# Sixteen projection blocks as seven products of quarter sums, in a stage of their own ahead of the pooling

## The chip, the cores and the metric

The kernel runs on one core of a Trainium2 chip. The metric is the device time of one execution in microseconds (us), from inputs in the chip's memory to the output there. Times are medians of several executions; a profile is one more execution, recorded by the hardware.

A core has TensorE (PE, matrix products into PSUM banks), VectorE (DVE), ScalarE (ACT), GpSimd (POOL) and SyncE (SP, which here issues all transfers). PEld is PE's loading of the stationary operand. An engine runs its own instructions in order and waits on semaphores for the others.

## What is computed

One transformer-like block over 1024 tokens of 1024 channels, with 16 learned meta tokens in front:

```python
u = rmsnorm(h, norm_mix)
z = u @ w_in                                   # 4112 columns
a, q, k, v, r, lr, ga, gb = split(z)           # 512, 256, 256, 512, 512, 16, 1024, 1024
p = (multiscale_pool(a) @ w_pool_mix) * pool_scale     # trailing means over 2, 4, 8, 16 tokens
y_a = p @ w_pool_out
log_a = log_sigmoid(lr @ w_gate_up + b_gate) / 16
o = gla_chunked(q / 8, k, v, log_a)            # gated linear attention, chunks of 64
y_b = (rmsnorm(o, gla_norm) * silu(r)) @ w_gla_out
m = sigmoid(ga) * y_a + sigmoid(gb) * y_b
h = h + m @ w_out
h = h + square(relu(rmsnorm(h, norm_ffn) @ w_ff1)) @ w_ff2
out = rmsnorm(h, norm_final)[16:]
```

## The kernel before

**Products.** Operands are float32, split into a rounded high part (an ACT copy) and a low part (a DVE subtraction). `mm3` makes one product from three matmuls per 128 rows of contraction: high x high, high x low, low x high. A direct block is 128 columns of a weight matrix against 512 tokens of either half: 8 x 3 matmuls for each half, 48 in all. Weight blocks come through the ring `W1`: `Ring.top_up` loads the next block into one of two raw buffers and splits it into one of two slots (`w1h`, `w1l`, each 1024 wide) as soon as the block that held the slot is done.

**Stages.** `start` (L368) normalizes eight tiles of 128 tokens and transposes them with PE (L239) into `TH`, `TL`, which hold the normalized tokens, channels on partitions, high and low, in two halves of 512 tokens (the meta tokens lead the first). The v projection of each tile (`v_tile`, 24 matmuls of 272 columns, with the 16 columns of lr) is woven in. Then come the pooling stage (four `a_block`, four `mix_block`, eight direct `ga_block`, four `ya_block` that multiply by the gates), the attention (`gla`), the output projection, and the two MLP layers.

**Attention.** `gla` runs four units (two pairs of heads, two halves). Each unit has a log decay (L659), six levels of masked scores (L707, a group of small matmuls; operands Q from DVE L732 and K from POOL L731, both times an exponential E from ACT; running sums in L674 and L675; the result merged by DVE L741) and then a state update across chunks. This chain uses PE little, so `pour` puts matmuls of a list of direct blocks, `fill`, between its steps: for every us that a step is expected to take, `PACE` us of filler. The filler before: k and q (2 blocks each), the second half of v, r (4), gb (8), and half of the GLA output projection.

**Seven products.** The first MLP layer already makes its blocks in pairs, 256 weight columns against all 1024 tokens, as a 2 x 2 by 2 x 2 product of quarters with seven quarter products in place of eight (the Strassen-Winograd scheme): P1, P2 on plain quarters, the other five on sums. A quarter product is 4 x 3 matmuls of 512 columns.

**Order.** PE's instructions stay in the order in which the code issues them. Those of the other engines are ordered by the scheduler of the framework.

## Time and profile before

| | us |
|---|---|
| median of 3 executions | 1280.34 (1279.92 to 1281.8) |
| the profiled execution | 1280.39 |
| its span in the profile | 1278.6 |

The page of the profile gives busy time by engine over the span, then the span in 40 slices, the chain of work that ended last, and groups of instructions that share a line, an engine and operands. In a group's row, "out<-in xcount | busy us, mean ns | idle before". PE's share in the chain that ended last is 85%, DVE's 5%. A matmul's duration overlaps its successor's, so PE's rate is read from starts or from busy time over count.

The slices that show where PE and DVE are busy (tenths, 40 slices of 32 us):

```profile
PE   5999999998999999999999999999999999999997
DVE  6446222262657664852797677677674777887686
ACT  6334334332355654430665445545553444444544
```

### The profile page before, as it was taken

The page shows a single profiled execution, that of the slowest core. Times are in us where ns is not written, and L with a number is a line of the kernel's source. Part 1 is how long each engine was busy: PE and PEld are TensorE (multiplying, and loading weights), DVE is VectorE, ACT ScalarE, POOL GpSimd, SP SyncE. Part 2 cuts the span into 40 slices and gives each one's busy share as a digit, 9 for nine tenths or more (in the row PEclk, how much of TensorE's full clock was granted, in tenths as well). Part 3 has the DMA queues.
Part 4 walks back from the last instruction along what each step waited for, and adds up shares of the span by engine and source line. Part 5 has one row for each costly group of instructions (what it writes and reads, how often), then busy time and mean ns, then how long its engine had stood idle before and what let it go on. Part 6 is the DMA issues. An engine that isn't in the chain of part 4 may idle for free.

```text
span 1278.6 us, 18111 instructions
## 1 busy us (share of the span) xinstructions
PE 1240.4 (97%) x6895; PEld 1020.3 (80%) x6895; DVE 798.5 (62%) x1295; ACT 590.5 (46%) x1045; POOL 78.8 (6%) x56
## 2 busy tenths in 40 slices
PE   5999999998999999999999999999999999999997
PEld 4988888887777788778878888888878788888776
DVE  6446222262657664852797677677674777887686
ACT  6334334332355654430665445545553444444544
POOL 1000001021111210520000000000000000000000
PEclk9999999998999999999999999999999999999999
DMA  8111223210032324880225445435559863333432
GB/s 237 49 33 50 83 83 100 67 33 17 26 108 89 103 93 129 272 308 31 84 99 175 159 130 165 160 130 165 167 196 355 288 239 108 99 91 91 166 92 90
DMA packets 138103, 164.92 MB, mean 129 GB/s; under 512 B 10368, under 2 KB 82832, under 8 KB 138016
## 3 DMA queue, kind: packets, MB, share of 16 engines
q1 hardware_dynamic: 138016, 163.76, 40.0%
q8 instruction: 54, 0.88, 0.3%
q14 instruction: 33, 0.27, 0.1%
HBM read 115.50 MB, written 48.23 MB: 128 GB/s over the span
## 4 chain that ended last, share of the span: by engine, by line
PE 85%; DVE 5%; issue 3%; DMA 3%; ACT 2%; POOL 0%; SPq 0%; DVEq 0%; POOLq 0%; ACTq 0%
PE b_mm L251 13%; PE b_mm L252 12%; PE b_mm L253 12%; PE b_o L252 8%; PE b_o L253 8%; PE b_o L251 8%; PE b_y L251 3%; PE b_y L253 3%; PE b_y L252 3%; PE b_sc L251 2%; PE b_sc L253 2%; PE b_z L251 2%; PE b_sc L252 2%; PE b_z L253 2%; PE b_z L252 2%
## 5 line engine op out<-in xcount | busy, mean ns | idle before, releaser
L251 PE MATMUL b_mm<-th,w1h 128*128 128x512 f32 (+1 forms) x496 | 188.4, 380 | 0.0
L252 PE MATMUL b_mm<-tl,w1h 128*128 128x512 f32 (+1 forms) x496 | 185.2, 373 | 0.0
L253 PE MATMUL b_mm<-th,w1l 128*128 128x512 f32 (+1 forms) x496 | 184.6, 372 | 0.0
L251 PEld LDWEIGHTS b_mm<-th,w1h 128*128 128x128 f32 x496 | 93.6, 189 | 20.9 <-issue 3.5
L76 DVE TENSOR_TENSOR w1l<-raw,w1h 128x1024 fp32r<-128x1024 f32 x38 | 50.7, 1335 | 91.4 <-ACT w1h L75 90.8
L253 PEld LDWEIGHTS b_mm<-th,w1l 128*128 128x128 f32 x496 | 93.7, 189 | 17.0
L252 PEld LDWEIGHTS b_mm<-tl,w1h 128*128 128x128 f32 x496 | 93.7, 189 | 15.5
L251 PE MATMUL b_o<-w1h 128*128 128x512 f32 x192 | 75.2, 392 | 2.7 <-DVE h L1154 1.7
L252 PE MATMUL b_o<-w1l,w1h 128*128 128x512 f32 x192 | 75.0, 391 | 1.2 <-DVE w1l L1008 1.2
L75 ACT ACTIVATE w1h<-raw 128x1024 fp32r<-128x1024 f32 x40 | 42.3, 1057 | 72.2 <-PE b_mm L252 72.2
L1007 ACT ACTIVATE w1h<-raw 128x512 fp32r<-128x512 f32 x88 | 54.7, 624 | 44.4 <-PE b_sc L252 14.1
L253 PE MATMUL b_o<-w1h,w1l 128*128 128x512 f32 x192 | 75.0, 391 | 0.1
L1008 DVE TENSOR_TENSOR w1l<-raw,w1h 128x512 fp32r<-128x512 f32 x88 | 60.2, 685 | 12.3 <-ACT w1h L1007 12.3
L483 DVE SCALAR_TENSOR_TENSOR t<-b_mm,t 128x512 f32<-128x512 f32 x40 | 27.6, 689 | 56.5 <-ACT t L482 56.1
L1202 DVE TENSOR_TENSOR bt<-w,w 128x512 f32<-128x512 f32 x80 | 54.8, 685 | 2.5 <-DMA w<-in_w_ff_dram 2.5
L1007 ACT ACTIVATE w1h<-bt 128x512 fp32r<-128x512 f32 x45 | 28.3, 630 | 57.1 <-issue 31.8
L251 PE MATMUL b_sc<-th,w1h 128*128 128x512 f32 x128 | 50.5, 394 | 0.7 <-ACT u2p L1126 0.7
L252 PE MATMUL b_o<-fxl,fxh 128*128 128x512 f32 x128 | 50.0, 391 | 0.7 <-DVE fxl L1008 0.7
L251 PE MATMUL b_mm<-wo,th 128*128 128x512 f32 x128 | 50.6, 396 | 0.0
L252 PE MATMUL b_z<-tl,w1h 128*128 128x512 f32 x128 | 49.9, 390 | 0.4 <-DVE tl L950 0.4
L251 PE MATMUL b_z<-th,w1h 128*128 128x512 f32 x128 | 49.9, 390 | 0.3 <-DVE h L1143 0.3
L253 PE MATMUL b_o<-fxh,fxl 128*128 128x512 f32 x128 | 50.2, 392 | 0.0
(289 smaller groups left out, 3072.6 us busy)
## 6 DMA issues: line engine op xcount, KB each, us to landing
hf_dram<-h SPq DMA_DIRECT2D x112, 256.0 KB, 2.1
raw<-hf_dram SPq DMA_DIRECT2D x112, 256.0 KB, 2.7
raw<-in_w_in_dram SPq DMA_DIRECT2D x32, 512.0 KB, 4.2
w<-in_w_ff_dram SPq DMA_DIRECT2D x64, 256.0 KB, 5.0
rawx<-in_w_ff_dram SPq DMA_DIRECT2D x16, 512.0 KB, 4.3
raw<-in_w_ff_dram SPq DMA_DIRECT2D x16, 512.0 KB, 4.2
xs<-in_x_dram SPq DMA_DIRECT2D x8, 512.0 KB, 5.7
ma_dram<-o SPq DMA_DIRECT2D x16, 256.0 KB, 2.0
```

The source lines that it names most:

```text
L75: self.nc.scalar.activation(hi, raw, ACT.Copy)
L76: self.eng.tensor_tensor(lo, raw, hi.bitcast(F32), ALU.subtract)
L251: pe.matmul(ps, ah, bh, start=first and i == 0, stop=False, skip_group_check=more)
L252: pe.matmul(ps, ah, bl, start=False, stop=False, skip_group_check=more)
L253: pe.matmul(ps, al, bh, start=False, stop=last and i == n - 1, skip_group_check=more)
L483: dve.scalar_tensor_tensor(t, b, 0.0, t, ALU.min, ALU.subtract)
L1007: act.activation(hi, a, ACT.Copy)
L1008: dve.tensor_tensor(lo, a, f32(hi), ALU.subtract)
L1202: dve.tensor_tensor(bt, w, S["w2"][q[3:]][:, i], ALU.add if q[2] == "+" else ALU.subtract)
```

## The change

The class `Quarters` now holds the seven-product scheme that the MLP's first layer had written out, with the weight blocks, their places and what is done with a result as arguments. It is used a second time, for sixteen blocks of `w_in`: all eight of ga, two of q, four of r and the first two of gb. They leave the pooling stage (ga) and the attention's filler (q, r, gb 0 and 1). Their results go to memory (`ga_dram`, `q_dram`, `r_dram`, `gb_dram`) and are loaded where they are used. P1, P2 of the first two pairs and v tiles are issued in `start`; the rest of the products in `gate_stage`, before the pooling.

The token side of five products needs differences of token quarters. `start` keeps a plain float32 copy `ut` of the transposed tiles (one more ACT copy from each transposed bank, L512), and `differences` makes the sums and their splits from these copies, 1024 columns an instruction.

In the pooling, the averages (`mean_block`) are parted from the mixing, groups run from 3 to 0, and the first `ya_block` starts with groups 3, 2, 1. `PACE` goes from 1.65 to 1.06, and POOL no longer splits weights in `start`.

```diff
-PACE, LEVEL = 1.65, 1.6
+PACE, LEVEL = 1.06, 1.6
-    banks(sc=1, mm=3, ms=3)
+    banks(sc=1, mm=2, ms=4)
...
+class Quarters:
+        def order(self):
+            for p, i in (("P1", 0), ("P2", 0), ("P1", 1), ("P2", 1), ("P5", 0), ("P5", 1)):
+                yield p, i
+            for p in ("P6", "P7", "P4", "P3"):
+                yield p, 0
+            for i in range(2, self.n + 1):
+                for p in ("P6", "P1", "P7", "P5", "P4", "P2", "P3"):
+                    m = i if p in ("P1", "P5", "P2") else i - 1
+                    if m < self.n:
+                        yield p, m
...
+        def prime(self):
+            w1 = [t.rearrange("p s (u c) -> p (s u) c", u=2) for t in (W1.hi, W1.lo)]
+            S["slots"] = [(w1[0][:, i], w1[1][:, i]) for i in range(4)]
+            self.made = ahead(self.forms(), 3)
...
+    BLOCKS = (
+        [("ga", d, C_GA + d * P) for d in range(8)] + [("q", p, C_Q + p * P) for p in range(2)]
+        + [("r", h, C_R + h * P) for h in range(HEADS)] + [("gb", d, C_GB + d * P) for d in range(2)]
+    )
...
+    def turned(u, t):
+        half, at = t // 4, OFF[t // 4] + (t % 4) * P
+        for j in range(2):
+            b = quad(bank("ms"))
+            for i in range(4):
+                pe.transpose(b[:, i], u[:, (4 * j + i) * P : (4 * j + i + 1) * P], ident)
+            k = slice(4 * j, 4 * j + 4)
+            split_from_psum(TH[half][:, k, at : at + P], TL[half][:, k, at : at + P], b)
+            act.activation(S["ut"][half, j][:, :, (t % 4) * P : (t % 4 + 1) * P], b, ACT.Copy)
...
     def start():
-        W1.eng = pool
+        for t in (1, 2, 3):
+            load(t)
+        q.load(0, 0)
         for t in range(8):
+            if t < 4:
+                layer_norm(xs[:, t % 4], us[:, t % 3])
+                turned(us[:, t % 3], t)
+                load(t + 4)
...
+                continue
+            if t == 4:
                 nc.sync.dma_start(xm, meta)
+                q.load(0, 1)
+                q.load(1, 1)
...
+                q.prime()
+                next(run)
+                next(run)
                 v_tile(0, 0)
+            layer_norm(xs[:, t % 4], us[:, t % 3])
+            turned(us[:, t % 3], t)
+            if t < 7:
+                v_tile(0, t - 3)
...
+        next(run)
         transposed(um, 0, 0)
+        next(run)
         v_tile(0, 8)
...
+    def halved(p, j):
+        h, l = gate_quarters.x[p] = [left.push(f"{p}{k}", [P, 4, HALF], F32R) for k in "hl"]
+        for k in range(0, 4, 2):
+            a = S["ut"][j][:, k : k + 2]
+            act.activation(h[:, k : k + 2], a, ACT.Copy)
+            dve.tensor_tensor(l[:, k : k + 2], a, f32(h[:, k : k + 2]), ALU.subtract)
+
+    def differences():
+        b11, b21, b12, b22 = (0, 0), (0, 1), (1, 0), (1, 1)
+        left.pop_to(S["left_x"])
+        differ(b11, b12, b11)
+        halved("P5", b11)
+        differ(b12, b22, b12)
+        differ(b22, b22, b11)
+        halved("P6", b22)
+        for t in range(4, 8):
+            v_tile(0, t)
+        lr_turn()
+        halved("P7", b12)
+        differ(b21, b21, b22)
+        halved("P4", b21)
...
+    def gate_result(i, w, b, u):
+        (kind, n, _), half = BLOCKS[2 * i + (w in (A12, A22))], int(w in (A21, A22))
+        if u is not None:
+            c = nxt("c")
+            dve.tensor_tensor(c, b, u, ALU.add)
+            b = c
+        o = nxt("o")
+        if kind == "q":
+            act.activation(o, b, ACT.Copy, scale=CH ** -0.5)
+            nc.sync.dma_start(q_dram[n, half], o)
+            return
+        t = sigmoid(b)
+        if kind == "r":
+            act.activation(t, t, ACT.Exp)
+            dve.scalar_tensor_tensor(o, b, gnorm[:, n : n + 1], t, ALU.mult, ALU.mult)
+            nc.sync.dma_start(r_dram[n, half], o)
+        else:
+            act.activation(o, t, ACT.Exp)
+            nc.sync.dma_start((ga_dram if kind == "ga" else gb_dram)[n, half], o)
...
-        (a_, 0), (a_, 1), (m_, 0), (a_, 2), (m_, 1), (a_, 3), (m_, 2), (g_, 0), (m_, 3), (g_, 1),
-        (y_, 0), (g_, 2), (g_, 3), (y_, 1), (g_, 4), (g_, 5), (y_, 2),
+        (a_, 3), (p_, 3), (a_, 2), (m_, 3), (p_, 2), (a_, 1), (m_, 2), (p_, 1), (a_, 0), (m_, 1), (p_, 0),
+        (y_, 0), (y_, 1), (y_, 2),
...
-        step(fill, q_block(p), W1, [w_cols(C_Q + p * P)])
-    for h in range(4):
-        step(fill, r_block(h), W1, [w_cols(C_R + h * P)])
-    for d in range(8):
+    for d in range(2, 8):
         step(fill, gb_block(d), W1, [w_cols(C_GB + d * P)])
```

Three places show how instructions move. First PE at the head of the program. Before, the first tile's eight transposes (into b_sc and b_ms) are followed by that tile's v matmuls (out b_mm, from the v weights vw and the tokens th, tl):

```order
L239 MATMUL b_sc<-ident,us 128x128 x4
L239 MATMUL b_ms<-ident,us 128x128 x4
L251 MATMUL b_mm<-vw_176,th_125 128x272
L252 MATMUL b_mm<-vw_176,th_125 128x272
L253 MATMUL b_mm<-vw_176,tl_129 128x272
```

Now the transposes of four tiles stand ahead of everything, and P1 of the first pair (out b_sc, weights w1h and w1l) follows:

```order
L509 MATMUL b_ms<-ident,us 128x128 x32
L253 MATMUL b_sc<-th_127,w1h 128x512
L254 MATMUL b_sc<-tl_131,w1h 128x512
L255 MATMUL b_sc<-th_127,w1l 128x512
L253 MATMUL b_sc<-th_127,w1h 128x512
```

24 matmuls of P1 and P2 moved ahead of the first v tile, and 24 transposes ahead of them. Behind them stand v tile 0, the transposes of tiles 4 to 7 with v tiles 1, 2, 3 between them, P1 and P2 of the second pair around the meta row's transposes, and v tiles 8, 4, 5, 6, 7.

Second, ACT where the first weight block of a direct projection is split (L75, from a raw buffer into w1h). Before, it stood inside the start, between the steps of a normalization (L225, L206) and the splits of a turned tile (L195):

```order
L225 ACTIVATE us,small<-xs 128x1024
L75 ACTIVATE w1h<-raw_109 128x1024
L206 ACTIVATE small<-small 128x1
L204 ACTIVATE small<-small 128x1
L351 ACTIVATE v_141<-b_mm 128x256
L195 ACTIVATE th_125<-b_sc 128x4x128
L75 ACTIVATE w1h<-raw_113 128x1024
```

Now it stands at the end of the products, among the sigmoids (L719 to L721, L626) of the last pair's results; raw_111 holds the first a-block's weights:

```order
L719 ACTIVATE t_851<-c 128x512
L720 ACTIVATE t_851<-t_851 128x512
L75 ACTIVATE w1h<-raw_115 128x1024
L721 ACTIVATE t_851<-t_851 128x512
L719 ACTIVATE t_851<-c 128x512
L720 ACTIVATE t_851<-t_851 128x512
L75 ACTIVATE w1h<-raw_111 128x1024
```

The first a-block's split moved to a place behind the second one's, which uses the other slot; its slot is one that the last product, P3 of the last pair, still reads.

Third, PE inside a level of the attention. Before, twelve filler matmuls stand between two score groups of the second unit (the last eleven, and the group behind them):

```order
L252 MATMUL b_mm<-tl_137,w1h 128x512
L253 MATMUL b_mm<-th_133,w1l 128x512
L251 MATMUL b_mm<-th_133,w1h 128x512
L252 MATMUL b_mm<-tl_137,w1h 128x512
L253 MATMUL b_mm<-th_133,w1l 128x512
L251 MATMUL b_mm<-th_133,w1h 128x512
L252 MATMUL b_mm<-tl_137,w1h 128x512
L253 MATMUL b_mm<-th_133,w1l 128x512
L251 MATMUL b_mm<-th_133,w1h 128x512
L252 MATMUL b_mm<-tl_137,w1h 128x512
L253 MATMUL b_mm<-th_133,w1l 128x512
L707 MATMUL b_sc<-Q,K 64x64 x16
```

Now nine stand there in the first unit, and in two places of the program none:

```order
L944 MATMUL b_sc<-Q,K 64x64 x16
L253 MATMUL b_mm<-th_135,w1h 128x512
L254 MATMUL b_mm<-tl_139,w1h 128x512
L255 MATMUL b_mm<-th_135,w1l 128x512
L253 MATMUL b_mm<-th_135,w1h 128x512
L254 MATMUL b_mm<-tl_139,w1h 128x512
L255 MATMUL b_mm<-th_135,w1l 128x512
L253 MATMUL b_mm<-th_135,w1h 128x512
L254 MATMUL b_mm<-tl_139,w1h 128x512
L255 MATMUL b_mm<-th_135,w1l 128x512
L944 MATMUL b_sc<-Q,K 64x64 x16
```

The second unit's log decays (L659) were followed by transposes (L770) and the state update (L778) with no filler between; now 72 matmuls of the second v projection stand behind those log decays.

More of the change, by code (lines that the diff above doesn't have):

```diff
@@ L253, in mm3, with quad, next_slot, split @@
             pe.matmul(ps, al, bh, start=False, stop=last and i == n - 1, skip_group_check=more)
+    def quad(a):
+        return a.rearrange("p (k c) -> p k c", k=4)
+    slot_n = [0]
+    def next_slot():
+        slot_n[0] += 1
+        return S["slots"][slot_n[0] % len(S["slots"])]
+    def split(a):
+        hi, lo = next_slot()
+        if len(a.shape) == 3:
+            hi, lo = quad(hi), quad(lo)
+        act.activation(hi, a, ACT.Copy)
+        dve.tensor_tensor(lo, a, f32(hi), ALU.subtract)
+        return hi, lo
@@ L287, in drive @@
         for ring, aps, fn in steps:
-            if fn is not start:
+            if fn not in (start, gate_stage):
                 for r in rings:
@@ L413, in start @@
         nc.sync.dma_start(wgu, w_gate_up)
+        for _ in S["gate_run"]:
+            pass
+        banks(keep=1, mm=3, ms=3)
     one = []
     step(one, start)
+    step(one, gate_stage)
     def pool_open():
@@ L690, in meta_state @@
         yield 1.0
+        while p and "v" not in done:
+            yield 1.0
         b = bank("ms")
@@ L994 @@
         step(one, out_tile(t, 1))
-    slot_n = [0]
-    def next_slot():
-        slot_n[0] += 1
-        return S["slots"][slot_n[0] % len(S["slots"])]
-    def split(a):
-        hi, lo = next_slot()
-        if len(a.shape) == 3:
-            hi, lo = quad(hi), quad(lo)
-        act.activation(hi, a, ACT.Copy)
-        dve.tensor_tensor(lo, a, f32(hi), ALU.subtract)
-        return hi, lo
-    def ahead(items, n):
-        made = []
-        for x in items:
-            made.append(x)
-            if len(made) > n:
-                yield made.pop(0)
-        yield from made
```

381 lines of the change are left out of this document (204 added, 177 removed).

## The prediction

> **What bounds the kernel now.** The page's first part comes first: which engine fills the span.
>
> ```profile
> span 1278.6 us, 18111 instructions
> PE 1240.4 (97%) x6895; PEld 1020.3 (80%) x6895; DVE 798.5 (62%) x1295; ACT 590.5 (46%) x1045; POOL 78.8 (6%) x56
> ```
>
> PE is busy in all but 38.2 us, so the time is PE's work plus its pauses. The profiled execution took 1280.39 us, 1.8 us more than its span and as good as the median of the runs, 1280.34; sums are made against 1280.4. Next the busy time of each engine in windows cut at the stages, for PE's pauses and granted clock.
>
> ```profile
> 0.00:57.90 57.90, 41.84 (x299) 39.31 (x300) 35.04 (x74) 31.03 (x71) 7.73 (x10) 0.97 0.56 157
> 57.90:237.00 179.10, 179.10 (x872) 150.86 (x872) 66.33 (x76) 71.51 (x111) 4.81 (x2) 1.00 0.23 67
> 253.00:309.00 56.00, 55.45 (x571) 49.16 (x570) 24.61 (x44) 17.64 (x42) 9.06 (x7) 1.00 0.08 20
> 309.00:375.00 66.00, 62.49 (x537) 47.88 (x537) 38.16 (x71) 30.92 (x59) 9.25 (x7) 0.92 0.20 61
> 375.00:480.00 105.00, 104.08 (x1018) 82.70 (x1018) 73.95 (x121) 64.83 (x114) 20.11 (x14) 1.00 0.31 96
> 660.00:940.00 280.00, 279.27 (x1226) 229.70 (x1225) 200.67 (x315) 141.72 (x237) 0.00 (x0) 1.00 0.46 151
> ```
>
> The columns are the window, then busy us and instructions of PE, PEld, DVE, ACT, POOL, then PE's clock and the DMAs. The start stage (to 57.9) loses 16 us; projections and pooling (to 237) lose nothing; the attention stage loses 0.5, 3.5 and 0.9. The pause near 309 also drops PE's clock to 0.92 over 66 us. The last row is the kernel's existing seven-product stage (first MLP layer): 1226 matmuls in 279.27 us, **0.2278 us each** for 512 columns, with DVE busy 72% and ACT 51% of it and PE never starved.
>
> **1. Removed: PE work.** Sixteen blocks took 16 x 48 matmuls, as eight pairs of 96. Now a pair takes 7 products x 12 = 84. 96 matmuls x 0.2278 = **-21.9 us**, all of it on the bounding engine. The rest of PE's list keeps its count.
>
> **2. The start stage.** P1 and P2 contract over all four token tiles of a half, so PE's first real product now waits until four tiles are normalized, turned and split; before, PE multiplied after the first tile.
>
> The timeline shows start, duration, engine and line, first PE's, then ACT's.
>
> ```profile
> 8.46 1.11 PE L239 MATMUL b_sc<-ident,us 128*128 128x128 f32 x4 [8.46 <-DVE us L227]
> ...
> 14.52 0.43 PE L253 MATMUL b_mm<-vw,tl 128*128 128x272 f32 x1
> ...
> 18.14 0.43 PE L251 MATMUL b_mm<-vw,th 128*128 128x272 f32 x1
> ...
> 22.14 0.29 PE L252 MATMUL b_mm<-vw,th 128*128 128x272 f32 x1
> ...
> 24.91 0.29 PE L253 MATMUL b_mm<-vw,tl 128*128 128x272 f32 x1
> ...
> 57.66 0.37 PE L251 MATMUL b_mm<-th,w1h 128*128 128x264 f32 x1
> ```
>
> ```profile
> 10.32 0.58 ACT L195 ACTIVATE th<-b_sc 128x512 fp32r<-128x512 f32 x1
> 10.80 0.59 ACT L195 ACTIVATE th<-b_ms 128x512 fp32r<-128x512 f32 x1
> ...
> 23.11 1.08 ACT L225 ACTIVATE us<-xs 128x1024 f32<-128x1024 f32 x1
> 24.06 0.22 ACT L225 ACTIVATION_READ_ACCUMULATOR us<-xs 128x1 f32 x1
> 24.16 1.08 ACT L75 ACTIVATE w1h<-raw 128x1024 fp32r<-128x1024 f32 x1
> ```
>
> From start to start of the ACT rows, a 512-wide ACT copy holds the engine 0.48 us, a 1024-wide square with its read-out 1.05, a 1024-wide copy about 0.95. Ahead of P1's last operand stand on ACT, after the first transposes (about 9.6): 8 splits and 6 plain copies of tiles (14 x 0.48 = 6.7), 4 squares (4.2), 4 weight splits (1.9), the v weights (2 x 0.95 + 0.3) and 10 one-column steps of about 0.25: 17.5 us, to 27; the low half on DVE puts P1 at **28**. PE is then continuous: v matmuls of 272 columns take 0.126 us warm (22.14 to 24.91 is 22 of them) and 0.226 cold (14.52 to 18.14 is 16). P1 and P2 of pair 0: 24 x 0.2278 = 5.5, plus 2.5 for starting cold (the 17 matmuls of the cold rows alone lost 1.7, and more stood on both sides of them); nine v tiles of 24: 27.2; transposes of tiles 4 to 7 and of the meta row 4.1; P1 and P2 of pair 1 5.5; the rank-16 turn 1.0, and 0.5 until its copy frees the bank for P5. Sum 46.3, so P5 starts at 74.3. Before, the same work stood at 57.66, plus the 48 products now in it (10.9) = 68.6. **+5.7 us**. Bounds: +1 if ACT and DVE reach P1 at 23, +12 if the transposes of tiles 4 to 7 wait as their like did before (4.1 us on L239, in the waits below) and P1 comes 2 us late.
>
> Two edits have no price of their own. Differences and splits of the four token quarters are 16 DVE operations of 1024 columns, 1.15 us each by the next rows (10.45 to 11.60), 18.4 us beside v tiles 4 to 7, P5 and P6 (24 us of PE); P7's operand is ready 1 us early, so up to 3 us if DVE is late. And the weight split leaves POOL, which stood beside a one-column DVE step of 2.36 us in place of 0.22; I count that in the start's sum only.
>
> ```profile
> 6.38 0.22 DVE L208 SCALAR_TENSOR_TENSOR small<-small 128x1 f32<-128x1 f32 x1 [0.47 <-ACT small L206]
> ...
> 10.45 1.23 DVE L325 TENSOR_TENSOR vw<-raw,vw 128x1024 fp32r<-128x1024 f32 x1 [2.05 <-ACT vw L323]
> 11.60 0.68 DVE L196 TENSOR_TENSOR tl<-b_sc,th 128x512 fp32r<-128x512 f32 x1
> ...
> 25.36 2.36 DVE L208 SCALAR_TENSOR_TENSOR small<-small 128x1 f32<-128x1 f32 x1
> ```
>
> The Trainium skill ("TensorE: Matmul & The Clock Gate", Part 1, the clock gate) says that PE runs at half clock until some 3.4 us of sustained work; by that P1's cold loss would be 1.7 us and the sum 0.8 lower. The rows' stretch, 3.6 us between its quoted ends alone, is the longer one, and the sum goes by it.
>
> **3. The products' steady state: 0.** A pair is 84 x 0.2278 = 19.1 us of PE.
>
> ```profile
> L1008 DVE TENSOR_TENSOR w1l<-raw,w1h 128x512 fp32r<-128x512 f32 x88 | 60.2, 685 | 12.3 <-ACT w1h L1007 12.3
> L1007 ACT ACTIVATE w1h<-raw 128x512 fp32r<-128x512 f32 x88 | 54.7, 624 | 44.4 <-PE b_sc L252 14.1
> L482 ACT ACTIVATE t<-t 128x512 f32<-128x512 f32 x40 | 25.2, 631 | 1.1
> ```
>
> ACT has 7 splits (0.62), one copy and 4 results of 4 steps (0.63): 15 us. DVE has 7 splits, 4 sums, 2 partial sums, 3 result sums and 4 sigmoid steps, 20 x 0.69 = 13.8, and 16.5 where r adds 4. Both fit in 19.1, and the MLP stage runs PE full with DVE at 72%. Bounds 0 to +5. The new stores and loads (ga and q to memory and back, 20 x 256 KB each way) meet a DMA share of 0.23 in 57.9 to 237; SP's queue puts weights of the pair after next behind results, with five products (11 us) in hand. If that is gone, a weight landing late costs about 4 us once.
>
> **4. From products to pooling: +2.4.** The first a-block's split reuses the slots of the very last product, so nothing can be split ahead (ACT rows of the change, above).
>
> First the waits of PE by what they waited for (total, times, longest), then two transposes of the start.
>
> ```profile
> PE b_sc L239 <- DVE tl L196: 4.1, 2, 3.1
> PE b_mm L253 <- DVE w1l L76: 2.1, 3, 1.2
> ...
> PE b_mm L251 <- ACT w1h L75: 0.8, 1, 0.8
> ```
>
> ```profile
> 32.22 1.11 PE L239 MATMUL b_sc<-ident,us 128*128 128x128 f32 x4 [3.12 <-DVE tl L196]
> ...
> 41.60 0.60 PE L239 MATMUL b_sc<-ident,us 128*128 128x128 f32 x4
> ```
>
> Split high 1.08, then low 1.15, plus handovers, less the two matmuls that need no low half: 2.4. The nearest wait of this kind (ring refilled at the output projection) shows 0.8 and 1.2. Bounds 1.5 to 4. A 3.1 us pause was followed by transposes of 1.11 in place of 0.60, so a pause not much longer than this one drops the clock; that would be 2 us more. The Trainium skill (the same page and part) lets the clock fall only after an idle window of about 3.4 us, and by it this pause keeps the clock.
>
> **5. Pooling: +1.1.** The averaging moves behind other a-blocks (at most five operations of 1.15 and two of 0.69, 7.1 us of DVE, against 11.4 of PE in an a-block: 48 x 0.122 + 24 x 0.2278). The last mix is consumed at once: its copy (0.48 to 0.58), low half (0.69) and handovers, less 0.7 of the second half's matmuls. Bounds 0 to 3.
>
> **6. Attention: -3.5.** Eight blocks (8 x 48 x 0.2278 = 87 us) leave the filler; the pace falls from 1.65 to 1.06 with it, so 9 matmuls (2.05 us) stand between score groups where 12 did (2.73). What is late next is the level chain on DVE and POOL.
>
> One level on DVE, POOL's part of it, and PE behind the pause at 309:
>
> ```profile
> 273.10 0.74 DVE L741 COPY_PREDICATED scc<-mask,b_sc 128x512 f32<-128x512 uint8 x1 [3.80 <-PE b_sc L707]
> 273.74 1.27 DVE L732 TENSOR_TENSOR Q<-q,E 128x512 f32<-128x512 f32 x1
> 275.55 0.43 DVE L674 TENSOR_TENSOR suf<-suf,pre 128x256 f32<-128x256 f32 x1 [0.54 <-ACT E L728]
> 276.08 0.43 DVE L675 TENSOR_TENSOR pre<-pre 128x256 f32<-128x256 f32 x1
> 276.69 0.75 DVE L741 COPY_PREDICATED scc<-mask,b_sc 128x512 f32<-128x512 uint8 x1 [0.19 <-PE b_sc L707]
> ```
>
> ```profile
> 273.17 1.29 POOL L731 TENSOR_TENSOR K<-k,E 128x512 f32<-128x512 f32 x1 [10.43 <-PE b_sc L707]
> ```
>
> ```profile
> 319.30 0.63 PE L251 MATMUL b_mm<-th,w1h 128*128 128x512 f32 x1
> 319.73 0.63 PE L252 MATMUL b_mm<-tl,w1h 128*128 128x512 f32 x1
> ```
>
> A level takes 3.4 of the 3.6 us here (273.10 to 276.69), 0.54 of it waiting for ACT, and only 0.19 for PE; Q takes 1.27 beside POOL's K, 0.68 elsewhere. With two buffers of Q and K it runs a level or two ahead, and 20 to 24 matmuls or a product of the other unit stand before most groups, so I charge 1 us at each of the two places where two groups now touch, and 2.5 for the handovers of four units (one of them cost the 0.9 in 375 to 480): 4.5. Against it goes the pause at 309 (all of 3.5, 0.5 and 0.9 above) and its tail: nine matmuls to 322 ran at 0.43 a start (1.8 us lost), and smaller ones before them, about 3 us. Now 72 v matmuls of 256 columns (8.5 us at 0.126 x 256/272) stand at that place, so 4.5 - 8 = -3.5. Bounds -8 to +18 (below).
>
> **Sum:** -21.9 + 5.7 + 0 + 2.4 + 1.1 - 3.5 = -16.2; 1280.4 - 16.2 = **1264**.
>
> **Rivals.** *The start costs more.* ACT holds 4.2 us a tile with the added plain copies, against 3.9 of PE, and waits for PE in turn. For: PE idled 16 us there already. Against: POOL's collisions go. Start +12, products +3: 1273. *The start costs nothing*, since products fill what were pauses: 1258 with the P5 handover free.
> *Slower: the level chain becomes the bound in attention.* It decides where less than 3.4 - 0.62 = 2.8 us of PE work stands between score groups. Some ten of 24 groups have 9 matmuls or fewer ahead (0.8 each, 8), two have none (5.6), and pauses that drop the clock as at 309 add 3: 16.6 in place of 4.5, and the 8 of the old pause come back elsewhere: 1264 + 20 = 1284. Against: the chain's lead, and DVE loses the eight blocks' sigmoids. The Trainium skill ("SBUF — State Buffer", section "SBUF: two separate sides") has a DVE operation with two SBUF inputs and a GpSimd one block each other for the whole instruction. Q at 1.27 beside K agrees with it, and by it no level gets under these 3.4 us. *The change does not do what it says*: if the stage's products ran at the direct blocks' cost, only +5.7 and the rest are left, 1286; PE's list, 96 matmuls shorter, speaks against it.
>
> **How the numbers follow.** Forecast (1258 to 1269) 0.62; dearer start or late products (1269 to 1277) 0.20; cheaper start (below 1258) 0.08; chain-bound attention 0.07, a good half of it above 1283; no saving 0.03. Range **1256 to 1277**: out of it fall the chain, no saving, and the ends of both start cases, about 2 in 10. A measurement here tells about 0.2%, 2.6 us. Faster 0.90, within 0.04, slower 0.06.
>
> **What would show it.** PE's instruction count falls by 96 with 0.228 a matmul unchanged. In the start: P1 near 28, P5 near 74. In the products: windows with PE full, else step 3 is wrong and the wait on PE names the split. At the end of the products one wait of PE for w1h and w1l of 2 to 3 us. In attention, no pause with a dropped clock; waits of PE for Q, K or the mask copy adding to over 10 us would make the slower rival right. A first product after 35, or PE waits for DMA, would break the forecast.

## The result and the profile after

The changed kernel takes **1288.13 us** (median of 4 runs, 1286.99 to 1290.79) against 1280.32 us, a ratio of 1.0058 (95% interval 1.0043 to 1.0073): slower by 0.6%. The forecast was 1264, 16 us faster. The profiled execution took 1286.99 us, so 22.8 us stand between forecast (1264.2 with the terms as they were) and measurement. They have to be found stage by stage.

First the page's engine row of the changed kernel.

```profile
span 1285.2 us, 18265 instructions
PE 1223.4 (95%) x6799; PEld 1006.1 (78%) x6799; DVE 881.1 (69%) x1425; ACT 623.4 (49%) x1117; POOL 72.1 (6%) x54
```

96 matmuls are gone, and PE's busy time fell by 17.0 us. But PE now idles 61.8 us (1285.2 - 1223.4) where it idled 38.2: 23.6 us more. The change did remove the work; the time was lost in pauses. The windows of the changed kernel, cut at its stages, show where (window, then busy us and instructions of PE, PEld, DVE, ACT, POOL, then PE's granted clock and the DMAs):

```profile
0.00:77.20 77.20, 54.33 (x346) 47.88 (x346) 53.59 (x101) 50.57 (x106) 1.26 (x7) 1.00 0.37 108
77.20:223.40 146.20, 144.92 (x624) 117.19 (x624) 101.14 (x153) 96.28 (x164) 0.00 (x0) 1.00 0.40 117
223.40:334.00 110.60, 108.37 (x582) 92.84 (x582) 52.64 (x59) 31.68 (x52) 6.11 (x3) 1.00 0.44 139
334.00:526.90 192.90, 174.53 (x1991) 143.03 (x1991) 136.93 (x242) 91.68 (x178) 46.50 (x33) 0.96 0.24 75
```

The rows are the start up to P5, the products behind it, the pooling, and the attention from PE's first log decay to the last transposes of its output. For the attention of the kernel before, the same cut:

```profile
253.80:511.80 258.00, 253.57 (x2341) 205.13 (x2342) 151.33 (x263) 127.92 (x233) 40.31 (x29) 0.98 0.24 74
```

PE's idle time in the attention rose from 4.4 to 18.4 us, and 4% of the clock was withheld over 193 us (some 7.7 us) in place of 2% over 258 (some 5.2). The fill work poured out here differs between kernels, so the exact account goes by what is left of the span after the first log decay. Before: 1278.6 - 253.8 = 1024.8 us, with eight direct blocks (48 x 0.2278 = 10.93 us each, 87.5 in all) that have gone to the front: 937.3 without them. After: 1285.2 - 334.0 = **951.2**. The attention was forecast to become 3.5 us cheaper, to 933.8; it is 17.4 dearer than that. The other 5.4 us lie ahead of it: the first log decay was due at 253.8 + 87.5 - 21.9 + 9.2 = 328.6 and came at 334.0. 5.4 + 17.4 = 22.8.

The same stretch, from the first log decay to the end, in both kernels:

```profile
253.80:1278.60 1024.80, 1003.23 (x5633) 816.06 (x5633) 693.79 (x1142) 484.33 (x858) 66.25 (x44) 0.99 0.43 139
```

```profile
334.00:1285.20 951.20, 915.75 (x5249) 748.20 (x5249) 673.68 (x1114) 444.90 (x798) 64.70 (x44) 0.99 0.43 142
```

Without the eight blocks' 87.5 us, PE is busy 915.8 us in either, and idle 21.6 before and 35.5 after. The 13.9 us between 937.3 and 951.2 are pauses; matmuls slowed by a lower clock would show as busy time, and over this stretch they cost about as much before as after.

**The front.** PE's timeline from P1 to the pooling (start, duration, engine, line; the idle time before it and who ended it): the first P1, the v tile behind its P2, the rank-16 turn, the first P5, P1 of two successive pairs, and the first a-block of the pooling.

```profile
27.75 0.79 PE L253 MATMUL b_sc<-th,w1h 128*128 128x512 f32 x1
...
37.01 0.29 PE L253 MATMUL b_mm<-vw,th 128*128 128x272 f32 x1
...
74.64 0.18 PE L479 MATMUL b_ms<-ident,lrtok 16*16 16x16 f32 x1
...
77.19 0.50 PE L253 MATMUL b_z<-P5h,w1h 128*128 128x512 f32 x1 [1.39 <-ACT gB L485]
...
108.37 0.40 PE L253 MATMUL b_sc<-th,w1h 128*128 128x512 f32 x1
...
127.83 0.40 PE L253 MATMUL b_sc<-th,w1h 128*128 128x512 f32 x1
...
223.41 0.39 PE L253 MATMUL b_mm<-th,w1h 128*128 128x264 f32 x1 [0.92 <-ACT w1h L75]
...
224.66 0.39 PE L255 MATMUL b_mm<-th,w1l 128*128 128x264 f32 x1 [0.75 <-DVE w1l L76]
```

P1 came as forecast (28), P5 2.9 us late (74.3). A pair takes 19.46 us (108.37 to 127.83), 0.2317 a matmul over its 84, where 0.2278 was taken from the MLP's products: 2.4 us over 624 matmuls. With 0.7 more at the stage's ends, the products were 3.1 over their sum (146.2 - 0.9 - 142.2). The hand-over cost its two waits, 1.7 (2.4 forecast), and the pooling came out within 0.1. 2.9 + 3.1 - 0.7 + 0.1 = 5.4.

**The attention.** What PE waited for, over the whole changed kernel (total us, times, longest):

```profile
PE b_sc L944 <- DVE scc L976: 7.5, 4, 2.7
PE b_m L1026 <- DVE S L1019: 6.4, 2, 4.0
...
PE b_m L1054 <- DVE on L1050: 2.0, 1, 2.0
PE b_sc L944 <- ACT scc L959: 1.3, 2, 1.0
```

In order: a score group waits for the mask copy of the level before; the products of scores and v wait for the end of the state chain; the last transposes wait for the normalized output; the first level's group waits for the copy on ACT. The first three are ends of chains on DVE. One such wait close up: DVE, POOL and PE of the changed kernel around 355 us, and the granted clock on both sides of the pause.

```profile
353.17 1.22 DVE L76 TENSOR_TENSOR w1l<-raw,w1h 128x1024 fp32r<-128x1024 f32 x1
354.30 0.42 DVE L909 TENSOR_TENSOR suf<-suf,pre 128x256 f32<-128x256 f32 x1
354.82 1.50 DVE L910 TENSOR_TENSOR pre<-pre 128x256 f32<-128x256 f32 x1
356.25 0.71 DVE L976 COPY_PREDICATED scc<-mask,b_sc 128x512 f32<-128x512 uint8 x1
```

```profile
354.78 1.26 POOL L966 TENSOR_TENSOR K<-k,E 128x512 f32<-128x512 f32 x1 [3.04 <-PE b_sc L944]
```

```profile
353.67 0.28 PE L255 MATMUL b_mm<-vw,tl 128*128 128x256 f32 x1
353.88 0.69 PE L944 MATMUL b_sc<-Q,K 64*64 64x64 f32 x32
357.10 1.13 PE L944 MATMUL b_sc<-Q,K 64*64 64x64 f32 x32 [2.53 <-DVE scc L976]
```

```profile
352.00:357.00 5.00, 2.58 (x49) 2.30 (x47) 4.90 (x8) 1.52 (x5) 1.26 (x1) 1.00 0.24 54
357.00:360.00 3.00, 2.90 (x40) 2.81 (x41) 2.23 (x3) 0.63 (x1) 1.28 (x1) 0.50 0.28 85
```

The group at 353.88 is done at 354.6. Its mask copy stands in DVE's queue behind a weight split of the filler (1.22) and both sums of the next level, and the second sum takes 1.50 us, where the first took 0.42, while POOL's K runs (e8 below shows that K is the reason). The copy comes at 356.25, the next group at 357.10: PE idles 2.53 us, and pays again, since the granted clock is 0.50 in the 3 us that follow. In the kernel before, fill work stood in this place.

### The profile page after: what moved, and what is told of

Same layout as the page of the kernel before. It is cut to its first block, busy times and chain, and to the rows that moved or that the text cites. A ratio compares the mean times of both kernels' runs of the same rounds, so it can differ in the third digit from the quotient of the medians.

```text
span 1285.2 us, 18265 instructions
## 1 busy us (share of the span) xinstructions
PE 1223.4 (95%) x6799; PEld 1006.1 (78%) x6799; DVE 881.1 (69%) x1425; ACT 623.4 (49%) x1117; POOL 72.1 (6%) x54
## 4 chain that ended last, share of the span: by engine, by line
PE 77%; DVE 10%; DMA 6%; ACT 4%; issue 2%; POOL 0%; SPq 0%; DVEq 0%; ACTq 0%; POOLq 0%
PE b_mm L253 7%; PE b_mm L254 7%; PE b_mm L255 7%; PE b_o L254 7%; PE b_o L255 7%; PE b_o L253 7%; PE b_y L253 5%; PE b_y L255 5%; PE b_y L254 5%; PE b_sc L253 3%; PE b_sc L254 3%; PE b_sc L255 3%; PE b_z L253 3%; PE b_z L254 3%; PE b_z L255 3%
## 5 line engine op out<-in xcount | busy, mean ns | idle before, releaser
L253 PE MATMUL b_mm<-th,w1h 128*128 128x512 f32 (+1 forms) x240 | 87.6, 365 | 0.9 <-ACT w1h L75 0.9
L255 PE MATMUL b_mm<-th,w1l 128*128 128x512 f32 (+1 forms) x240 | 85.0, 354 | 0.7 <-DVE w1l L76 0.7
L254 PE MATMUL b_mm<-tl,w1h 128*128 128x512 f32 (+1 forms) x240 | 85.2, 355 | 0.0
L254 PE MATMUL b_sc<-tl,w1h 128*128 128x512 f32 x192 | 76.0, 396 | 0.3 <-DVE tl L198 0.3
L255 PE MATMUL b_sc<-th,w1l 128*128 128x512 f32 x192 | 75.9, 396 | 0.0
L271 ACT ACTIVATE w1h<-fs 128x512 fp32r<-128x512 f32 x72 | 45.4, 630 | 49.9 <-PE b_y L254 34.4
L255 PE MATMUL b_z<-th,w1l 128*128 128x512 f32 x160 | 62.3, 389 | 0.0
L272 DVE TENSOR_TENSOR w1l<-fs,w1h 128x512 fp32r<-128x512 f32 x72 | 49.3, 685 | 16.5 <-ACT w1h L271 16.5
L253 PEld LDWEIGHTS b_mm<-th,w1h 128*128 128x128 f32 x240 | 46.1, 192 | 10.2 <-issue 2.3
L255 PEld LDWEIGHTS b_mm<-th,w1l 128*128 128x128 f32 x240 | 46.3, 193 | 7.1 <-DVE w1l L76 1.0
```

The lines of the kernel that those rows point to most:

```text
L253: pe.matmul(ps, ah, bh, start=first and i == 0, stop=False, skip_group_check=more)
L254: pe.matmul(ps, ah, bl, start=False, stop=False, skip_group_check=more)
L255: pe.matmul(ps, al, bh, start=False, stop=last and i == n - 1, skip_group_check=more)
L271: act.activation(hi, a, ACT.Copy)
L272: dve.tensor_tensor(lo, a, f32(hi), ALU.subtract)
```

## The experiments

**Theory 1:** the attention's chains (levels, state, normalization) were covered by the filler and now lie bare, and the pauses cost clock too. **Rival:** the loss was made elsewhere, in the start and the products. The kernel before ran again beside each group of kernels (1281.22 us beside e1 to e4, 1280.95 beside e5 to e8, 1282.73 beside e9 to e12), and each ratio is to those runs; kernels of different groups are best compared by their ratios. Below, "rest" is the span less the time of the first log decay, less 10.93 us for each direct block (q, r, gb 0, gb 1) that is in it: what the attention and all behind it cost with the moved blocks left out. Spans are those of the one profiled execution, which lies up to 2.2 us from the median (e4: 1286.82 against 1284.65), so differences of 2 us in rest are not told apart.

| kernel | median us (runs) | ratio to before, 95% | first log decay | span | rest |
|---|---|---|---|---|---|
| before | 1280.32 (4) | | 253.8 | 1278.6 | 937.3 |
| changed | 1288.13 (4) | 1.0058 (1.0043 to 1.0073) | 334.0 | 1285.2 | 951.2 |
| e1 before, thin filler | 1294.27 (2) | 1.0102 (1.0073 to 1.0131) | 342.4 | 1292.5 | 950.1 |
| e2 pace 1.45 | 1295.53 (2) | 1.0112 (1.0082 to 1.0141) | 335.9 | 1293.9 | 958.0 |
| e3 early v | 1286.90 (4) | 1.0044 (1.0024 to 1.0064) | 332.4 | 1286.1 | 953.7 |
| e4 ga only | 1284.65 (8) | 1.0020 (1.0006 to 1.0033) | 257.5 | 1285.0 | 940.0 |
| e5 r back | 1272.18 (4) | 0.9932 (0.9895 to 0.9969) | 294.1 | 1271.4 | 933.6 |
| e6 two score places | 1289.12 (5) | 1.0053 (1.0029 to 1.0077) | 336.0 | 1288.0 | 952.0 |
| e7 copies on POOL | 1290.32 (3) | 1.0078 (1.0041 to 1.0114) | 336.4 | 1288.0 | 951.6 |
| e8 K on DVE | 1279.66 (8) | 0.9999 (0.9979 to 1.0018) | 333.8 | 1275.7 | 941.9 |
| e9 before, K on DVE | 1281.87 (10) | 0.9997 (0.9987 to 1.0006) | 254.4 | 1279.2 | 937.3 |
| e10 r back, K on DVE | 1270.94 (4) | 0.9913 (0.9888 to 0.9938) | 294.2 | 1270.4 | 932.5 |
| e11 and early v | 1269.36 (4) | 0.9890 (0.9865 to 0.9915) | 291.4 | 1267.2 | 932.1 |
| e12 gb back, K on DVE | 1275.14 (4) | 0.9939 (0.9917 to 0.9961) | 317.2 | 1274.9 | 935.8 |

**e1: the thin filler alone, without any products.** The kernel before, its eight blocks taken ahead of the attention:

```diff
-PACE, LEVEL = 1.65, 1.6
+PACE, LEVEL = 1.06, 1.6
...
+    for p in range(2):
+        step(fill, q_block(p), W1, [w_cols(C_Q + p * P)])
+        told(("q", p))
+    for h in range(4):
+        step(fill, r_block(h), W1, [w_cols(C_R + h * P)])
+        told(("r", h))
+    for d in range(2):
+        step(fill, gb_block(d), W1, [w_cols(C_GB + d * P)])
     for p in range(2):
         step(fill, k_block(p), W1, [w_cols(C_K + p * P)])
...
-        yield 3.6
+        yield 4.4
```

> The kernel before, with nothing of the products in it: its eight direct blocks q, r, gb 0 and gb 1 are only taken ahead of the attention's first unit, and pace and order of the filler are those of the changed kernel. All of its work is done, in another order. Theory 1 (the change lost its gain in the attention, because a filler 87 us thinner leaves the level chain and the state chain of the scan bare, and the pauses drop PE's clock as well): PE's pauses and lost clock in the attention rise from 9.7 us to about 25, as in the changed kernel, so 1280.4 + 14 = about 1294 (1290 to 1298). Rival (the attention is no worse for it; the loss was made in the start and the products, or by q, r and gb coming back from memory): 1279 to 1283.

Measured 1294.27 us. The attention window of e1, and the pauses of PE in it:

```profile
342.40:535.60 193.20, 174.38 (x1990) 143.22 (x1991) 137.97 (x242) 91.75 (x178) 46.82 (x33) 0.96 0.24 75
```

```profile
365.76 1.14 PE L711 MATMUL b_sc<-Q,K 64*64 64x64 f32 x32 [2.52 <-DVE scc L745]
...
407.18 0.70 PE L711 MATMUL b_sc<-Q,K 64*64 64x64 f32 x32 [2.65 <-DVE scc L745]
...
484.39 3.37 PE L795 MATMUL b_m<-v,scc 64*64 64x128 f32 x30 [4.02 <-DVE S L788]
...
534.78 1.07 PE L823 MATMUL b_m<-ident,on 128*128 128x128 f32 x8 [1.98 <-DVE on L819]
```

And those of the changed kernel behind the one at 357.10:

```profile
397.23 0.69 PE L944 MATMUL b_sc<-Q,K 64*64 64x64 f32 x32 [2.65 <-DVE scc L976]
...
475.98 3.09 PE L1026 MATMUL b_m<-v,scc 64*64 64x128 f32 x30 [4.02 <-DVE S L1019]
...
526.08 1.06 PE L1054 MATMUL b_m<-ident,on 128*128 128x128 f32 x8 [1.97 <-DVE on L1050]
```

Pause for pause the two lists agree, 8.4 to 10.0 us apart in time and within 0.01 us in length. A kernel without products, with the changed kernel's filler, has the changed kernel's attention: 950.1 against 951.2. The rival falls for the attention's part: neither the products nor q coming back from memory is needed for this loss.

**e2: the filler spent faster.** `PACE` 1.45 in place of 1.06.

> The changed kernel with the pace of the filler at 1.45 in place of 1.06, nothing else. The filler of the first three rounds is 95 us (second k block, v, six gb blocks) and the steps of these rounds ask for 64 us times the pace, so 1.06 left some 27 us of it to be poured out behind, where there is nothing to cover. Theory 1 (bare chains in the attention): about 37% more PE work stands at each step, pauses and lost clock in the attention fall from 25 us to about 13 to 18, so 1288 falls to 1277 to 1282. Rival (the waits are on chains so long that a step's share does not matter, or were made elsewhere): 1286 to 1290.

Measured 1295.53 us, 7 worse, against both. The expectation overlooked the last two rounds: they ask for 39 us times the pace, and behind the 95 us only the four yb blocks are left, 20 us by their own costs. So the filler is worth 115 us in all and is asked for 103 times the pace, 109 at 1.06 and 149 at 1.45; the 27 us were no surplus. Two windows of e2, parted at 496 us:

```profile
335.90:496.00 160.10, 154.20 (x1647) 126.26 (x1647) 109.75 (x197) 84.97 (x164) 40.79 (x27) 1.00 0.26 80
496.00:542.30 46.30, 26.77 (x369) 22.69 (x370) 36.54 (x57) 14.60 (x22) 13.65 (x9) 0.72 0.39 126
```

Up to 496 the denser filler does what theory 1 says, 5.9 us idle in 160 and a full clock; then it is used up, and 46 us hold 19.5 us of pauses at a clock of 0.72. The amount of filler counts, and 1.06 uses up nearly all of it (109 of 115) over the whole attention.

**e3: three v tiles ahead of P1.**

```diff
                 load(t + 4)
+                if t:
+                    v_tile(0, t - 1)
...
-                v_tile(0, 0)
+                v_tile(0, 3)
...
-            if t < 7:
-                v_tile(0, t - 3)
+            if t < 6:
+                next(run)
+            elif t == 6:
+                v_tile(0, 4)
...
```

> The changed kernel with three v tiles of the start moved ahead of P1 of the first pair, into the time in which PE waits for the tiles, and P1 and P2 of the second pair moved to where v tiles stood. If the start's loss (P5 at 77.2 us in place of 74.3 as forecast and 68.6 before) is PE idling until P1 at 27.75: three v tiles of 3.0 us leave the full stretch, P1 moves by at most 2 us for their copies on ACT, P5 comes at 69 to 72, and the time falls by 5 to 8 us, to 1280 to 1283. Rival (ACT or DVE sets the start's end, PE's order does not matter): P5 stays within 2 us of 77.2 and the time within 2 us of 1288.

```profile
33.74 0.39 PE L253 MATMUL b_sc<-th,w1h 128*128 128x512 f32 x1
...
74.95 0.51 PE L253 MATMUL b_z<-P5h,w1h 128*128 128x512 f32 x1 [1.66 <-ACT gB L485]
```

P1 moved 6.0 us back, P5 came 2.2 us earlier, and the median fell by 1.2 us, within the spread of the runs. The first log decay came 1.6 us earlier, and the rest behind it came out 2.5 larger, little more than these spans can tell. Neither the 5 to 8 us nor the rival's zero: the first v tile had to wait for its weights until 20.17 us, so only part of PE's pause could be used.

**e4 and e5: give the attention its filler back.** In e4 only ga stays as products, all eight other blocks are direct again with the pace and waits of before; in e5 only r returns:

```diff
-PACE, LEVEL = 1.06, 1.6
+PACE, LEVEL = 1.4, 1.6
...
-        + [("r", h, C_R + h * P) for h in range(HEADS)] + [("gb", d, C_GB + d * P) for d in range(2)]
+        + [("gb", d, C_GB + d * P) for d in range(2)]
...
     told("v")
+    for h in range(4):
+        step(fill, r_block(h), W1, [w_cols(C_R + h * P)])
+        told(("r", h))
     for d in range(2, 8):
...
```

> The changed kernel with only the eight ga blocks as products (four pairs); q, r, gb 0 and gb 1 are direct blocks in the attention's filler again, with the pace, order and waits of before. 48 matmuls of 0.2278 us come back (+10.9 us of PE). Theory 1: the attention's pauses and lost clock go back from 25 us to about 10 as before, so 1288 + 11 - 14 = about 1285 (1282 to 1288). Rival (the attention's filler does not matter, the loss is in start and products): 1288 + 11 = 1297 to 1300, less what four pairs fewer lose in the products' steady state (2 of 4 us).

> The changed kernel with the four r blocks as direct blocks in the attention's filler again, six pairs (ga, q, gb 0 and gb 1) as products, pace 1.4 (the filler's 121 us becomes about 162). 24 matmuls come back (+5.5 us of PE). Theory 1 (the attention's loss goes with the PE work that stands at each step): half of the filler back gives about half of the 15 us back or somewhat more, 7 to 10, so 1288 + 5.5 - 8.5 = about 1285 (1282 to 1287). Rival (the loss goes away only when all eight blocks are back): 1291 to 1294.

e4 took 1284.65 us, as theory 1 had it; its rest went back to 940.0, in an execution 2.2 us above the median. It also shows what the front costs by itself. Its first log decay came at 257.5 in place of 253.8, though four pairs save 48 matmuls (10.9 us) ahead of it: the front is 14.6 us dearer than its work. In the changed kernel it is the same 14.6 (334.0 against 253.8 + 87.5 - 21.9 = 319.4), with twice the pairs. So most of this is an entry cost (forecast 9.2), and four pairs do not earn it: e4 is 0.2% slower than the kernel before.

e5 took **1272.18 us**, far under what either side expected, and under the kernel before. The attention window of e5:

```profile
294.10:515.30 221.20, 216.66 (x2184) 176.13 (x2185) 147.75 (x263) 114.94 (x215) 48.63 (x32) 0.98 0.27 83
```

PE idles 4.5 us there, as before the change. Four blocks, poured at pace 1.4, give back all the cover that eight gave at 1.65, and the rest is 933.6. The loss is not in proportion to the filler, as theory 1 had been priced for e5; the chains are covered from some point between none and four blocks. Below it four blocks in the filler are worth 17.6 us of rest (15.0 of them pauses of PE behind the first log decay, 35.5 to 20.5), while as products they save 24 matmuls, 5.5 us.

**e6: successive score groups in alternating halves of their banks.**

```diff
-        b = two("sc")[:, :, : 4 * CH].rearrange("p e (j t) -> p e j t", j=4)
+        sc_n[0] += 1
+        b = two("sc")[:, :, sc_n[0] % 2 * 4 * CH :][:, :, : 4 * CH].rearrange("p e (j t) -> p e j t", j=4)
```

> The changed kernel with the score groups of successive levels in alternating halves of the two PSUM banks, so that a group need not wait for the mask copy of the level before. Theory 1a (the wait of score groups for the mask copy, 7.5 us in four waits and 1.3 for the first copy, is the handing back and forth of one buffer): these waits fall below 3 us and part of the lost clock with them, 1288 falls to 1278 to 1283. Rival 1b (the chain of DVE work itself, mask copy, Q and the two sums of a level, is what a group waits for): the waits stay at 6 to 9 us in sum under another name (Q or K), 1286 to 1290.

Measured 1289.12 us, but it tells nothing of the two sub-theories. In e6's trace a mask copy (L977) starts at 397.44 and takes 0.71; the score group (L945) that waited 2.65 us for it starts at 398.30. The group still starts 0.15 us behind the end of the copy, though it no longer writes what the copy reads. The waits for the mask copy stayed, 6.5 us in three, under their old name. The edit did not take the wait away, and why it stayed is not shown; whether a second score buffer would help is open.

**e7: the plain copies on POOL**, as sums of the high and low halves.

```diff
-            act.activation(S["ut"][half, j][:, :, (t % 4) * P : (t % 4 + 1) * P], b, ACT.Copy)
+            th, tl = (f32(a[half][:, k, at : at + P]) for a in (TH, TL))
+            pool.tensor_tensor(S["ut"][half, j][:, :, (t % 4) * P : (t % 4 + 1) * P], th, tl, ALU.add)
```

> The changed kernel with the plain copies of the token quarters made on POOL as the sum of the high and low halves already in SBUF, in place of 16 ACT copies out of PSUM. If ACT sets P1 in the start (its 17.5 us of work ahead of P1 hold 8 such copies, 3.8 us): P1 comes at 24 in place of 27.75, P5 at 73.5 in place of 77.2, the time falls by 3 to 4 us to about 1284. Rival (DVE, which splits and normalizes, sets it, and is slowed beside POOL): P1 at 27.5 or later, 1288 to 1292.

```profile
25.30 0.79 PE L253 MATMUL b_sc<-th,w1h 128*128 128x512 f32 x1
27.51 0.79 PE L254 MATMUL b_sc<-tl,w1h 128*128 128x512 f32 x1 [1.41 <-DVE tl L198]
```

P1's first matmul came 2.5 us earlier, its second, which needs DVE's low half, only 1.3 (28.84 in the changed kernel), P5 came no earlier (77.97), and the time was 1290.32. ACT's copies did hold P1's first matmul; the next to hold it is DVE's low half, with POOL at work beside it.

**e8: K of the levels on DVE.** The close-up above names POOL's K as what slows the second sum.

```diff
-            pool.tensor_tensor(kl, k, e, ALU.mult)
+            dve.tensor_tensor(kl, k, e, ALU.mult)
             dve.tensor_tensor(ql, q, e, ALU.mult)
```

> The changed kernel with K of each level made on DVE in place of POOL. A Q beside POOL's K took 1.27 us and 0.68 alone, so Q and K one after the other should take 1.36 on DVE. If DVE and POOL only take turns, a level costs DVE the same and the time stays within 3 us of 1288. If POOL's K does carry part of the chain (K and Q ready together after 1.3 us while DVE goes on to the sums), the waits of the attention grow by 24 levels times up to 0.3 us, to 1290 to 1295.

Measured 1279.66 us: 8.5 less than the changed kernel (7.6 by the two ratios), which neither side expected. Groups of the changed kernel (24 levels; busy us and mean ns of one), then of e8:

```profile
L966 POOL TENSOR_TENSOR K<-k,E 128x512 f32<-128x512 f32 x24 | 34.0, 1415 | 135.9 <-PE b_sc L944 63.5 <-ACT E L964 37.8 <-DVE suf L909 28.4
...
L910 DVE TENSOR_TENSOR pre<-pre 128x256 f32<-128x256 f32 x24 | 21.1, 877 | 1.5 <-ACT E L964 0.3
L967 DVE TENSOR_TENSOR Q<-q,E 128x512 f32<-128x512 f32 x24 | 20.1, 836 | 0.3 <-ACT E L964 0.3
```

```profile
L967 DVE TENSOR_TENSOR Q<-q,E 128x512 f32<-128x512 f32 x24 | 17.6, 732 | 0.0
...
L966 DVE TENSOR_TENSOR K<-k,E 128x512 f32<-128x512 f32 x24 | 16.4, 684 | 1.5 <-PE b_ms L1005 0.9 <-ACT E L964 0.6
...
L910 DVE TENSOR_TENSOR pre<-pre 128x256 f32<-128x256 f32 x24 | 10.2, 423 | 1.0
```

K took 1.42 us on POOL and held DVE's sums and Qs up meanwhile (pre 0.88 against 0.42). On DVE it takes 0.68 and the others run undisturbed, so pre, Q and K together take 1.84 us of DVE a level where pre and Q alone took 1.71, and what stands behind pre in DVE's queue no longer waits for POOL. The same pause as in the close-up, on e8's PE, then e8's attention window and its waits of the kinds listed for the changed kernel:

```profile
355.43 0.69 PE L944 MATMUL b_sc<-Q,K 64*64 64x64 f32 x32 [1.34 <-DVE scc L976]
```

```profile
333.80:518.50 184.70, 173.07 (x1990) 140.77 (x1991) 132.65 (x266) 91.97 (x178) 13.31 (x9) 0.97 0.26 79
```

```profile
PE b_sc L944 <- DVE scc L976: 5.8, 3, 2.6
...
PE b_m L1026 <- DVE S L1019: 2.4, 2, 1.8
```

2.53 became 1.34, with the clock at 1.00 behind it (355 to 358), and the attention's idle time is 11.6 in place of 18.4. The close-up was the best case, though: the mask copy's waits fell only from 7.5 to 5.8 us in all, and the larger part came at the end of the state chain, 6.4 to 2.4. That chain's steps (L1019, 0.34 us each) stand in the same DVE queue as the sums of the levels that POOL's K had stretched. The Trainium skill ("SBUF — State Buffer", section "SBUF: two separate sides") has a DVE operation with two SBUF inputs and a GpSimd operation take an exclusive lock on a shared port pair, for the whole instruction, first come first served. The trace agrees: pre, started at 354.82 beside a K of 354.78, took 1.50 us: the 0.42 that it takes alone, and most of K's 1.26.

**e9: the same edit in the kernel before**, to see whether e8's gain is the chain's or POOL's in general.

> The kernel before, with K of each level on DVE in place of POOL, nothing else. In the changed kernel this edit gave 8.4 us. If it did so because the level chain lies bare there (theory 1), it gives little where a filler of eight more blocks covers the chain: 0 to 3 us, 1277.5 to 1280.5. Rival (a K on POOL lengthens DVE's operations, and that costs about the same in any kernel): 6 to 8 us, 1272 to 1275.

```profile
254.40:510.40 256.00, 252.12 (x2340) 204.10 (x2341) 151.03 (x287) 127.33 (x233) 7.32 (x5) 0.99 0.24 75
```

1281.87 us, ratio 0.9997 (0.9987 to 1.0006), and the rest is 937.3 as without the edit. Under the thick filler a shorter chain is worth nothing that these runs can tell; under the thin one it is worth about 8 us. That is theory 1 from its other side.

**e10 to e12: the parts put together.** e10 is e5 with e8's edit, e11 adds e3's. e12 returns gb 0 and gb 1 alone (seven pairs as products, pace 1.2), with e8's edit.

> Six pairs as products, the four r blocks in the filler (1272.2 us in the look before this one), and K on DVE. Theory 1: the filler covers the chain there already (3.6 us of pauses left in the attention), so K on DVE gives 0 to 3 us more: 1269 to 1272. Rival (the two gains add up): 1264 to 1266.

> As the kernel with r in the filler and K on DVE, with the three early v tiles of the start too, which brought P5 2.2 us forward. If that is carried through to the end, as nothing in the products waits: 2 us less than without, 1267 to 1270. If the wait only comes later in the start's DVE work: no difference.

> Seven pairs as products, only gb 0 and gb 1 back in the filler, pace 1.2, K on DVE: one pair more than with r back, so 12 matmuls (2.7 us) fewer, and 22 us of filler less. Theory 1 with a shorter chain: what stands at each step (pace 1.2) about covers a level without POOL, so pauses of 3 to 6 us more than with r back, 1269 to 1274. If two blocks do as four did: 1266 to 1268.

1270.94, **1269.36** and 1275.14 us. With r back, K on DVE gives 1.2 us by the medians and 2.4 by the ratios, as little as theory 1 said and within the spread of the runs; e11's further 1.6 is of the size expected, and within the spread too. e12 lies 1.1 above its range. e11 beats the kernel before by 1.1% (interval 0.85 to 1.35). e12's rest (935.8) is 3.3 above e10's, as two blocks less would have it; its front is 3.5 us later than e10's plus one pair (294.2 + 19.5). PE waits there 1.7 us at the hand-over and 1.3 for the result of a `ya_block` on DVE; e10's trace has neither.

## Why the prediction was wrong, point by point

- **1, removed work:** right. 96 matmuls left PE's list.
- **2, the start:** right in kind, 2.9 us too small. P1 came at 27.75 as worked out. P1 and P2 of the first pair took 9.26 us from start to start (27.75 to 37.01; 8.0 charged), the rank-16 turn with P5's wait 2.55 (74.64 to 77.19; 1.5 charged), and the tiles and P1, P2 of the second pair made the rest. Two tries to pack the stage tighter met the next wait: with v tiles early (e3) PE waits for their weights, with ACT relieved (e7) for DVE.
- **3, steady state:** PE waited only once there (0.4), as forecast, but a matmul came at 0.2317 us in place of 0.2278; with the ends 3.1 us in place of 0, inside the bounds of 0 to +5. A rate taken from another stage did not hold here.
- **4 and 5:** 1.7 in place of 2.4; the pooling within 0.1 of its sum.
- **6, attention: the step that failed.** It said that a Q and K buffer of two let the level chain run "a level or two ahead", that 20 to 24 matmuls stand before most groups, and charged 4.5 us for new waits against 8 gained from the old pause at 309. The gain came for the most part: at that pause's place (3.5 us before) the changed kernel waits 0.36 and 0.74 us, at a clock of 1.00 (366 to 380). The charge failed: the new waits are 17.2 us, and the clock fell again behind the three longest of them. In the trace the mask copy stands in DVE's queue behind the sums of the next level and behind weight splits, so a score group cannot run ahead of it (7.5, with 1.3 at the first copy); the state chain (6.4) and the normalization (2.0) had no price at all. e1 shows that the thin filler does this by itself, and e5 that half of the filler prevents it. e5's rest, 933.6, is the forecast's 933.8, but e5 is another kernel (four blocks still in the filler, pace 1.4), so that is no check of the two terms.
- **The rivals:** the slower one, "the level chain becomes the bound in attention", is about half of the mechanism that happened. It was priced at 1284 and given 0.07. It put waits at twelve score groups and had the old pause come back; waits came at four groups, 1.1 to 2.7 us each, the old pause did not, and its price left out the state chain and the front's 5.4 us. That 1284 lies near 1288 is in part luck. Against it stood "the chain's lead", which no row had shown.
- **What would show it:** the mark "waits of PE for Q, K or the mask copy adding to over 10 us" pointed at the right stage, but it was not reached: the mask copy's waits are 7.5 us, 8.8 with the first copy. Only with the state chain (6.4) and the output (2.0), which it did not name, do the waits come to 17.2. The mark "no pause with a dropped clock" did tell.

## What to carry to other kernels

Work that an engine does while it would otherwise wait for a chain hides that wait. Before moving or shrinking such work, count what the chains need, every one that shares the in-order queue (here levels, state and normalization, all on DVE), and keep enough of it: here it was enough with four of the eight moved blocks kept (pace 1.4), and not with none of them (1.06). A change that removes work should take it from the stage that has nothing to hide: here twelve blocks as products ahead, with four left as filler, gave the gain that sixteen did not. A new stage also has an entry cost (here some 14 us), and what it saves must exceed it: eight blocks alone did not. And an operation handed to a second engine to relieve the first should be timed together with what it slows there.

## What the runs showed of the hardware

- PE's clock fell behind pauses of 2.53, 2.65 and 4.02 us: the granted clock was 0.50 from 357 to 360, 0.50 from 398 to 401 and 0.57 from 476 to 479 in the changed kernel. Behind pauses of 2.39 (at 432.67) and 1.97 (at 526.08) it stayed at 1.00. The Trainium skill ("TensorE: Matmul & The Clock Gate", Part 1, the clock gate) lets it fall after an idle window of about 3.4 us; by that the two shorter ones keep the clock. Between the end of the last full matmul (353.67 + 0.28) and the group at 357.10 lay 3.15 us with one 64x64 score group in it, still less than that window, even if such a group did not count as work. The clock also fell with no such pause: it was 0.62 from 336 to 338 and 0.53 from 338 to 340, among full matmuls that had run since 335.02, behind the log decays' small matmuls (16 rows) and a pause of 0.89. So the length of a pause alone does not tell here whether the clock falls.
- A sum of 256 columns on DVE took 1.50 us beside a product on POOL and 0.42 without, so giving a product to POOL spared DVE next to nothing: 0.13 us a level in pre and Q.
- The same kind of matmul came every 0.2278 us in the MLP stage and every 0.2317 in the new one, though in both stages PE was busy nearly throughout (a wait of 0.4 us in the new one, at 1.00 of the clock); why is open.
